# Two projections of a mixer on a seven-product scheme, woven between plain column groups, with four attention heads in one row

## The chip, the cores and the metric

The kernel runs on one core of one Trainium2 chip. The metric is device time in microseconds (us) of one execution, lower is better. The time of the kernel before is the median of three runs.

## The reference

One layer of an encoder with 256 tokens and a model width of 2048, all in float32:

```python
x = layer_norm(ALPHA * x + 0.5 * swiglu(x, ffn1_w1, ffn1_w3, ffn1_w2))
mix = hybrid_mixer(x, w_in, ...)
x = layer_norm(ALPHA * x + mix)
x = layer_norm(ALPHA * x + 0.5 * swiglu(x, ffn2_w1, ffn2_w3, ffn2_w2))
x = x + sigmoid(x @ w_ple_gate) * (p @ w_ple_proj)
```

The mixer multiplies x by one wide matrix `w_in` (2048 rows) and cuts the result into columns: q, k, v and the output gate of an mLSTM (1024 columns each, 4 heads of 256), 8 columns for the mLSTM's input and forget gates, q, k, v of a stick-breaking attention (1024 columns each, 8 heads of 128) and two merge gates (2048 columns each). The mLSTM's q and k go through a causal convolution over four tokens and a silu. Each mLSTM head forms decayed scores of 256 x 256 tokens, multiplies them by v, divides by a normaliser (the row sum of the scores, bounded below), normalises the head, and multiplies by the sigmoid of the output gate. Both branches are then projected up, gated, added and projected out.

## The kernel before

**Matmuls.** A float32 weight tile of 256 rows x 512 columns (512 KB, called raw) is loaded by SP's DMA queue, and split by ScalarE and VectorE into a high part (`nc.scalar.copy`, line 1024) and a low part (`nc.vector.tensor_tensor`, line 1028) of a reduced-precision type that TensorE multiplies fast. The activations, transposed, exist as high and low part too (`ActT`). A product of one weight tile with one half of the tokens is a `Unit`: for each of the tile's two blocks of 128 rows three matmuls of 128 x 512 (lines 1073 to 1075: high x high, high x low, low x high), so six matmuls for each unit.

**Plain groups.** `group` makes the units of one column group: 512 columns, 8 weight tiles over the 2048 rows, and each tile is used for both token halves, so 16 units, accumulated in two PSUM banks.

**Seven products.** `seven` (line 295) treats two column groups and two token halves and two row halves as a 2 x 2 block product and forms it by 7 products in place of 8, in Winograd's form. It needs sums of activation blocks (`act.forms`, made by `form_turn`, line 261), and sums of weight blocks. Some sums are made while loading, by a second DMA on POOL's queue that adds to the tile (line 1001), others by VectorE (`plus`, line 310). For 2048 rows it has 28 units, each with a weight tile of its own: products 1 and 2 first, with four units each, then four rounds of products 5, 7, 6, 4 and 3, whose five PSUM banks stay open over all four rounds. In the kernel before only the two feed-forward parts use it: 8 of their 11 chunks are made so (`up7`), and their units are woven (`weave`) between the plain units of the other work.

**The mixer.** Its projections are all plain groups, in this order: q group 0, the gates with the first two stick-breaking heads' q (264 columns), q group 1, k 0, k 1, v 0, v 1, output gate 0 and 1, then the stick-breaking columns in portions of 4, 4, 4, 4, 4 and 2 heads (`sb_columns`), the merge gates (`branch`), the two up-projections (`ups`), and the projection out. `conv` turns a finished q or k group: 4 transposes, then ScalarE's and VectorE's steps (line 690) that read PSUM. `sb_turn` (line 601) transposes a finished portion of stick-breaking q or k. `mlstm(h)` and `stick(h)` are the steps of one attention head. They are generators: each step is put into the engines' programs when its due time, counted in units already emitted, has come (`Sched`). The mLSTM's heads run as two sequences side by side, (0, 1) and (2, 3); a head waits for gates, q, k and v at its start, and for the output gate before its last steps (line 769). The row sum of the scores comes from a column of ones behind v: the matmul at line 754 has 257 columns.

**What sets the order.** Each engine runs its program in the order in which the Python code emitted it. The weights ahead of the matmuls are bounded by two numbers: raw tiles held (8 in the feed-forward parts, 5 in the mixer, 4 near a boundary) and split tiles held (6, near a boundary 11). Raw tiles, split halves, activations and the large intermediate values share one pool of 44 pages of 4 KB in each partition (`PAGES`); a raw tile takes one page, a split tile two. Short-lived values use 6 temporary buffers (`TEMP_BUFS`): if none is free, the code emits pending steps ahead of their due time. All matmul results use 8 PSUM banks (`PSUM_BUFS`).

Of the kernel before, what the change touches and what calls it, by code (L numbers as in the profile page):

```python
# [13 lines left out]
P = 128  # L14
S = 256
TT = S // P
D = 2048
# [120 lines left out]


class Boundary:  # L140


    def __init__(self, mixer):
        self.mixer = mixer


def weave(main, side):
# [22 lines left out]
def kernel(  # L170
# [121 lines left out]
                               i == 0, i == len(rows) - 1, done) for t in range(TT)])  # L292
        return pairs

    def seven(wa, wb, rows, col0, cols, act, done):

        n = rows // (4 * P)
        accs = {m: {} for m in range(1, 8)}

        def unit(m, i, tile, src, half, sub):
            return Unit(tile, half, accs[m], src, i, sub, i == 0, i == n - 1, lambda ps, t, m=m: done(m, ps))

        def plus(out, a, b):
            def make():
                nc.vector.tensor_tensor(out=out.tile[:, :, :cols], in0=a.tile[:, :, :cols], in1=b.tile[:, :, :cols],  # L310
                                        op=ALU.add)
            return make

        units = []
        for m, sub in ((1, 0), (2, 2)):
            for i in range(n):
                units.append(unit(m, i, plain(rows_of(wa, (4 * i + sub) * P, col0, cols)), act, 0, sub))
        for i in range(n):
            b11, b12, b22, b21 = (rows_of(w, (4 * i + sub) * P, col0, cols)
                                  for w, sub in ((wa, 0), (wb, 0), (wb, 2), (wa, 2)))  # L320
# [12 lines left out]
    program = []  # L333

    def boundary(mixer):
        program.append(Boundary(mixer))


    class Norm:
# [96 lines left out]
    def ffn(w1, w3, w2, act, norm, skew=True, ahead=()):  # L436
# [22 lines left out]
        def up7(c):  # L459
# [46 lines left out]
                return  # L506
                yield

            return seven(w1, w3, D, c * COL, COL, act, done)

        def down(*chunks):
            pairs = []
# [20 lines left out]
        boundary(True)  # L533


    xT = ActT(act_tile, ActT(act_tile))
# [13 lines left out]
    flags = set()  # L550

    def mixer_setup():
        st["sel"] = big()[0:HM, 0:HM * P].rearrange("q (h s) -> q h s", s=P)
        nc.vector.memset(st["sel"], 1.0)
        nc.gpsimd.affine_select(st["sel"], st["sel"], pattern=[[-1, HM], [0, P]], compare_op=ALU.is_equal,
                                fill=0.0, base=0, channel_multiplier=1)
        raw = temp()
        nc.sync.dma_start(out=raw[0:64, 0:P], in_=conv_m[0].rearrange("j (b q) -> (j b) q", q=P))
        st["cw"] = small.tile([P, 64], F32, name="cw", bufs=1)
        st["bi"] = small.tile([HM, 1], F32, name="bi", bufs=1)  # L560
        st["bf"] = small.tile([HM, 1], F32, name="bf", bufs=1)
        bg = b_gates_m[0].rearrange("(a h) -> a h", h=HM)
        nc.sync.dma_start(out=st["bi"][:], in_=bg[0].rearrange("(h o) -> h o", o=1))
        nc.sync.dma_start(out=st["bf"][:], in_=bg[1].rearrange("(h o) -> h o", o=1))

        def later():
            yield DELAY["gb"]
            ps = misc([P, 64])
            nc.tensor.transpose(ps[:], raw[0:64, 0:P], ident[0:64, 0:64])
            nc.vector.tensor_copy(out=st["cw"][:], in_=ps[:])  # L570
            drop()
            flags.add("cw")
        sched.spawn(later())
# [122 lines left out]
            yield DELAY["cv2"]  # L696
        drop(2)

    def v_done(g):
        def done(ps, t):  # L700
            st["v", t, g] = big()[:, 0:2 * (DM + 1)].rearrange("q (h d) -> q h d", d=DM + 1)
            nc.vector.memset(st["v", t, g][:, :, DM:], 1.0)
            nc.scalar.copy(st["v", t, g][:, :, 0:DM], ps.rearrange("q (h d) -> q h d", d=DM))
            flags.add(("v", t, g))
        return done
# [5 lines left out]
    def mo_done(g):  # L711
        def done(ps, t):
            if ("mo", t) not in st:
                st["mo", t] = big()
            cs = slice(g * COL, (g + 1) * COL)
            activate(st["mo", t][:, cs], ps, ACT.Sigmoid)
            nc.gpsimd.tensor_tensor(out=st["mo", t][:, cs], in0=st["mo", t][:, cs],
                                    in1=st["nm"][:, cs], op=ALU.mult)
            flags.add(("mo", t, g))
        return done  # L720

    ymT, ysbT = ActT(act_tile), ActT(act_tile)

# [1 line left out]
        return tl[:, 0:512].rearrange("q (a s) -> q a s", s=S)[:, :, 0:P]  # L725

    def mlstm(h):
        yield from wait("gates", ("qk", 0, h), ("qk", 1, h), ("v", 0, h // 2), ("v", 1, h // 2))
        d = temp()
        ps = misc([P, S])  # L730
        nc.tensor.matmul(ps[:], st["sel"][:, h], st["M"], start=True, stop=True)
# [18 lines left out]
        for t in range(TT):  # L750
            ps = misc([P, DM + 1])
            for s in range(t + 1):
                off = s * 256 + (t - s) * P
                nc.tensor.matmul(ps[:], d[:, off:off + P], st["v", s, h // 2][:, h % 2], start=(s == 0), stop=(s == t))  # L754
# [82 lines left out]
    first = 2  # L837
    for n in (4, 4, 4, 4, 4, 2):
        program.extend(flat(group(w_in, range(0, D, 2 * P), sq0 + first * DS, n * DS, x1T,
                                  lambda ps, t, f=first, n=n: sb_columns(ps, t, f, n))))  # L840
        first += n
        if first == 18:
            program.append(lambda: [sched.spawn(in_sequence([stick(a), stick(a + 2), stick(a + 4), stick(a + 6)]))
                                    for a in (0, 1)])


    mergedT = ActT(act_tile)
# [57 lines left out]
        if g == 1:  # L905
            program.append(norm2.load)

    boundary(False)


    x3T = ActT(act_tile)
# [55 lines left out]

    warm(WARM)

    weights, edges = [], []  # L970
    for u in program:
        if isinstance(u, Boundary):
            edges.append((len(weights), u.mixer))
# [6 lines left out]

    def limits(j):

        if any(-EDGE <= j - e < EDGE for e, _ in edges):
            return RAW_EDGE, SPLIT_EDGE
        mixer = [m for e, m in edges if e <= j][-1:] == [True]
        return (RAW_MIX, SPLIT_MIX) if mixer else (RAW_FFN, SPLIT_FFN)

    def pieces(j):
        return [slice(0, 1), slice(1, 2)] if j == 0 else [slice(0, 2)]
# [63 lines left out]
    splits_due()  # L1053
    warm(WARM2)
    for u in program:
        if isinstance(u, Boundary):
            continue
        if not isinstance(u, Unit):
            u()
# [51 lines left out]
```

## Time and profile before

| | |
|---|---|
| median of 3 runs | 2207.83 us (2206.65 to 2209.06) |
| the profiled execution | 2207.09 us, of which the span in the profile is 2205.4 us |
| TensorE's granted clock | 1.000 |
| TensorE matmul busy | 2196.6 us (100% of the span) |
| VectorE busy | 1747.1 us (79%) |
| ScalarE busy | 1244.5 us (56%) |
| GpSimd busy | 118.9 us (5%) |
| moved by DMA | 543.85 MB, mean 247 GB/s |

The profile lists engines as PE (matmul), PEld (TensorE's weight load), DVE (VectorE), ACT (ScalarE), POOL (GpSimd) and SP (the queue that issues most DMAs). Matmuls are pipelined: a row's duration is longer than the distance to the next one, and TensorE counts as busy when it only works below its peak. L1074 is line 1074 of the kernel.

### The profile page before, as it was taken

To read this page: it belongs to the slowest core of one execution; us is meant where nothing else is said; L and a number is where in the kernel's file an instruction comes from. 1 tells how busy PE (TensorE), PEld (TensorE's weight loads), DVE (VectorE), ACT (ScalarE), POOL (GpSimd) and SP (SyncE) were. 2 spreads that over 40 slices of the span, in tenths; PEclk is the share of its full clock that TensorE was granted. 3 is DMA by queue.
4 is the path that set the end of the run, shared out by engine and by line. 5 is a ranking of instruction groups with operands and counts; after the bars stand their busy time and mean duration, and the time that the engine had idled before them with its cause. 6 is when DMAs were issued, how large, how long until landed. Compare 5 with 4: busy or idle time off the path is not lost.

```text
span 2205.4 us, 27919 instructions
## 1 busy us (share of the span) xinstructions
PE 2196.6 (100%) x10062; PEld 1819.0 (82%) x10062; DVE 1747.1 (79%) x1923; ACT 1244.5 (56%) x1505; POOL 118.9 (5%) x111
## 2 busy tenths in 40 slices
PE   9999999999999999999999999999999999999999
PEld 7888888888888888888888888888888888887888
DVE  6999999999987874654445456699999999989774
ACT  7556656565655555545643344656565565656372
POOL 0100010000000000000100000000010001000000
PEclk9999999999999999999999999999999999999999
DMA  9899999999993765655566666579989999999553
GB/s 334 246 312 299 283 283 318 303 308 275 320 315 115 217 199 158 190 164 167 158 190 187 187 225 218 183 230 303 303 265 306 324 287 298 288 301 336 200 165 104
DMA packets 284811, 543.85 MB, mean 247 GB/s; under 512 B 17120, under 2 KB 26240, under 8 KB 284672
## 3 DMA queue, kind: packets, MB, share of 16 engines
q1 hardware_dynamic: 262912, 500.12, 68.3%
q0 software_dynamic: 21760, 41.95, 11.0%
q8 instruction: 79, 1.29, 0.2%
q14 instruction: 60, 0.49, 0.1%
HBM read 539.90 MB, written 2.10 MB: 246 GB/s over the span
## 4 chain that ended last, share of the span: by engine, by line
PE 94%; DVE 2%; DMA 2%; issue 1%; ACT 0%; SPq 0%; DVEq 0%; POOLq 0%; ACTq 0%
PE mm L1074 30%; PE mm L1073 30%; PE mm L1075 30%; DMA raw<-in_ffn_w_dram 2%; DVE split L1028 1%; PE ms L249 1%; PE ms L392 0%; DVE raw L310 0%; PE ms L791 0%; PE ms L814 0%; PE ms L742 0%; PE ms L754 0%; PE ms L804 0%; ACT split L1024 0%; DVE actT L256 0%
## 5 line engine op out<-in xcount | busy, mean ns | idle before, releaser
L1028 DVE TENSOR_TENSOR split<-raw,split 128x1024 fp32r<-128x1024 f32 (+1 forms) x1013 | 1177.6, 1201 | 237.8 <-ACT split L1024 225.3
L1024 ACT CAST split<-raw 128x1024 fp32r<-128x1024 f32 (+1 forms) x1013 | 1007.0, 1036 | 496.9 <-DVE raw L310 139.5
L1073 PE MATMUL mm<-split,actT 128*128 128x512 f32 (+2 forms) x3152 | 1226.9, 389 | 0.5 <-DVE xres L516 0.5
L1074 PE MATMUL mm<-split,actT 128*128 128x512 f32 (+2 forms) x3152 | 1215.1, 386 | 1.4 <-DVE split L1028 1.3
L1075 PE MATMUL mm<-split,actT 128*128 128x512 f32 (+2 forms) x3152 | 1215.1, 386 | 0.6 <-DVE actT L256 0.6
L1074 PEld LDWEIGHTS mm<-split,actT 128*128 128x128 f32 x3152 | 592.8, 188 | 120.3 <-DVE split L1028 6.1
L1075 PEld LDWEIGHTS mm<-split,actT 128*128 128x128 f32 x3152 | 592.2, 188 | 121.0 <-DVE actT L256 1.4
L1073 PEld LDWEIGHTS mm<-split,actT 128*128 128x128 f32 x3152 | 592.6, 188 | 117.0 <-issue 1.0
L310 DVE TENSOR_TENSOR raw<-raw 128x1024 f32<-128x1024 f32 x176 | 214.6, 1219 | 1.9
L1001 POOL DMA_DIRECT2D raw<-in_ffn_w_dram x80 | 95.9, 1198 | 1415.7 <-DMA raw<-in_ffn_w_dram 404.1
L251 ACT CAST actT<-ms 128x512 fp32r<-128x512 f32 x60 | 35.0, 585 | 89.4 <-PE ms L249 88.4
L463 DVE TENSOR_TENSOR temp<-mm,temp 128x512 f32<-128x512 f32 x112 | 76.7, 685 | 6.4 <-PE mm L1075 4.6
L516 DVE SCALAR_TENSOR_TENSOR xres<-mm,xres 128x512 f32<-128x512 f32 x96 | 65.3, 684 | 15.9 <-PE mm L1075 15.8
L256 DVE TENSOR_TENSOR actT<-ms,actT 128x512 fp32r<-128x512 f32 x60 | 40.9, 683 | 24.6 <-ACT actT L251 13.7
L221 ACT ACTIVATE big<-mm 128x512 f32<-128x512 f32 x20 | 12.0, 598 | 55.8 <-PE mm L1075 55.8
L221 ACT ACTIVATE temp<-temp 128x512 f32<-128x512 f32 (+1 forms) x48 | 28.5, 593 | 23.8 <-DVE temp L806 22.0
L221 ACT ACTIVATE temp<-mm 128x512 f32<-128x512 f32 (+1 forms) x22 | 12.3, 560 | 45.5 <-PE mm L1075 45.4
L217 ACT ACT_TABLE_LOAD x29 | 37.2, 1283 | 0.5
L244 DVE TENSOR_TENSOR actT<-temp,actT 128x512 fp32r<-128x512 f32 x32 | 21.4, 688 | 17.3 <-ACT actT L243 17.2
L861 DVE TENSOR_TENSOR big<-mm,big 128x512 f32<-128x512 f32 x16 | 11.1, 692 | 30.0 <-PE mm L1075 30.0
L690 DVE SCALAR_TENSOR_TENSOR temp<-ms,cw,temp 128x253 f32<-128x253 f32 (+2 forms) x48 | 23.1, 481 | 7.4 <-ACT temp L221 6.2
L221 ACT ACTIVATE rstd<-mv,eps 128x1 f32<-128x1 f32 x6 | 1.8, 295 | 46.4 <-DVE mv L375 46.4
(124 smaller groups left out, 542.1 us busy)
## 6 DMA issues: line engine op xcount, KB each, us to landing
raw<-in_ffn_w_dram SPq DMA_DIRECT2D x655, 512.0 KB, 6.5
raw<-in_w_in_dram SPq DMA_DIRECT2D x168, 512.0 KB, 3.8
raw<-in_ffn_w_dram POOLq DMA_DIRECT2D x80, 512.0 KB, 8.9
raw<-in_w_out_dram SPq DMA_DIRECT2D x32, 512.0 KB, 5.3
raw<-in_w_ple_gate_dram SPq DMA_DIRECT2D x24, 512.0 KB, 4.8
raw<-in_w_up_m_dram SPq DMA_DIRECT2D x16, 512.0 KB, 3.9
raw<-in_w_up_sb_dram SPq DMA_DIRECT2D x16, 512.0 KB, 4.4
raw<-in_w_ple_gate_dram SPq DMA_DIRECT2D x16, 256.0 KB, 4.4
```

The costliest lines, as they stand in the source:

```text
L217: nc.scalar.preload_act_table_set(table[0])
L221: nc.scalar.activation(out, in_, func, **kw)
L256: nc.vector.tensor_tensor(out=dst[:, 1], in0=ps[:], in1=dst[:, 0], op=ALU.subtract)
L310: nc.vector.tensor_tensor(out=out.tile[:, :, :cols], in0=a.tile[:, :, :cols], in1=b.tile[:, :, :cols], op=ALU.add)
L463: nc.vector.tensor_tensor(out=out, in0=a, in1=b, op=op)
L516: nc.vector.scalar_tensor_tensor(out=xs, in0=ps, scalar=0.5, in1=xs, op0=ALU.mult, op1=ALU.add)
L1001: nc.gpsimd.dma_start(out=r.tile[:, :, :r.cols], in_=r.plus, accum_op=ALU.add)
L1024: nc.scalar.copy(hi[:, ks], r[:, ks])
L1028: nc.vector.tensor_tensor(out=lo[:, ks], in0=r[:, ks], in1=hi[:, ks], op=ALU.subtract)
L1073: nc.tensor.matmul(ps, hi, w[0][:, k, :u.cols], start=first, stop=False)
L1074: nc.tensor.matmul(ps, hi, w[1][:, k, :u.cols], start=False, stop=False)
L1075: nc.tensor.matmul(ps, lo, w[0][:, k, :u.cols], start=False, stop=last)
```

## The change

The mLSTM's v and output gate are made by `seven`, each as one call for both of its column groups, in place of four plain groups. The 56 units are woven between the plain units of q 1, k 0, k 1 and the first three stick-breaking portions, in that ratio (96 to 56). For this the normalised activations `x1T` get the sums of blocks (`forms`), so the norm keeps whole copies of them. In this stretch 7 raw tiles are held in place of 5. `both7` combines the seven products into the result's four blocks, in pages of their own.

The mLSTM's four heads become one sequence, and each waits for its output gate at its start. Since v now lies in a page without room for the column of ones, the row sum comes from matmuls of their own with one column of `ones`, on the same scores. The selection matrix `sel` is replaced by a broadcast column of the identity.

```diff
-RAW_FFN, RAW_MIX, RAW_EDGE = 8, 5, 4
-SPLIT_FFN, SPLIT_MIX, SPLIT_EDGE = 6, 6, 11
+HELD = {"ffn": (8, 6), "mix": (5, 6), "wide": (7, 6)}
+RAW_EDGE, SPLIT_EDGE = 4, 11
...
-    def seven(wa, wb, rows, col0, cols, act, done):
+    def seven(wa, ca, wb, cb, rows, cols, act, done):
...
+    def both7(w, ca, cb, act, dest, ready):
+
+        r, held = {}, {}
+
+        def put(k, t, a, b, op):
+            nc.vector.tensor_tensor(out=r[k, t], in0=a, in1=b, op=op)
+
+        def rest():
+            u = r[0, 1]
+            put(0, 1, held[7], u, ALU.add)
+            z = r[1, 1] = dest(1, 1)
+            nc.vector.scalar_tensor_tensor(out=z, in0=u, scalar=-1.0, in1=held[5],
+                                           op0=ALU.mult, op1=ALU.subtract)
+            ready(1, 1)
...
+        def done(m, ps):
+            held[m] = ps
+            if m == 1:
+                r[0, 1] = dest(0, 1)
+                nc.scalar.copy(r[0, 1], ps)
+            elif m == 2:
+                r[0, 0] = dest(0, 0)
+                put(0, 0, ps, r[0, 1], ALU.add)
+                ready(0, 0)
+            elif m == 6:
+                r[1, 0] = dest(1, 0)
+                put(0, 1, ps, r[0, 1], ALU.add)
+                put(1, 0, held[5], r[0, 1], ALU.add)
+                sched.spawn(rest(), DELAY["rest"])
+            elif m == 4:
+                sched.until(lambda: (1, 1) in r)
+                put(0, 1, ps, r[0, 1], ALU.add)
+                ready(0, 1)
+            elif m == 3:
+                put(1, 0, ps, r[1, 0], ALU.subtract)
+                ready(1, 0)
+
+        return seven(w, ca, w, cb, D, COL, act, done)
...
-    x1T = ActT(act_tile)
+    x1T = ActT(act_tile, ActT(act_tile))
...
-        st["sel"] = big()[0:HM, 0:HM * P].rearrange("q (h s) -> q h s", s=P)
-        nc.vector.memset(st["sel"], 1.0)
-        nc.gpsimd.affine_select(st["sel"], st["sel"], pattern=[[-1, HM], [0, P]], compare_op=ALU.is_equal,
-                                fill=0.0, base=0, channel_multiplier=1)
...
+    def v_dest(g, t):
+        if ("v", t) not in st:
+            st["v", t] = big()
+        return st["v", t][:, g * COL:(g + 1) * COL]
...
+    def mo_ready(g, t):
+        a = mo_dest(g, t)
+        activate(a, a, ACT.Sigmoid)
+        nc.gpsimd.tensor_tensor(out=a, in0=a, in1=st["nm"][:, g * COL:(g + 1) * COL], op=ALU.mult)
+        flags.add(("mo", t, g))
...
     def mlstm(h):
-        yield from wait("gates", ("qk", 0, h), ("qk", 1, h), ("v", 0, h // 2), ("v", 1, h // 2))
+        yield from wait("gates", ("qk", 0, h), ("qk", 1, h), ("v", 0, h // 2), ("v", 1, h // 2),
+                        ("mo", 0, h // 2), ("mo", 1, h // 2))
...
-        nc.tensor.matmul(ps[:], st["sel"][:, h], st["M"], start=True, stop=True)
+        nc.tensor.matmul(ps[:], ident[0:HM, h:h + 1].broadcast_to([HM, P]), st["M"], start=True, stop=True)
...
-                nc.tensor.matmul(ps[:], d[:, off:off + P], st["v", s, h // 2][:, h % 2], start=(s == 0), stop=(s == t))
+                nc.tensor.matmul(ps[:, 0:DM], d[:, off:off + P], st["v", s][:, h * DM:(h + 1) * DM],
+                                 start=(s == 0), stop=(s == t))
+            for s in range(t + 1):
+                off = s * 256 + (t - s) * P
+                nc.tensor.matmul(ps[:, DM:], d[:, off:off + P], ones[:, 0:1], start=(s == 0), stop=(s == t))
...
-        yield from wait(("mo", 0, h // 2), ("mo", 1, h // 2))
...
+    program.append(load_norm_m)
+    program.append(lambda: sched.spawn(in_sequence([mlstm(a) for a in range(HM)])))
+    main = []
     for which, g in ((0, 1), (1, 0), (1, 1)):
-        program.extend(flat(group(w_in, range(0, D, 2 * P), which * 1024 + g * COL, COL, x1T, qk_done(which, g))))
-    program.append(load_norm_m)
-    program.append(lambda: [sched.spawn(in_sequence([mlstm(a), mlstm(a + 1)])) for a in (0, 2)])
-    for g in range(2):
-        program.extend(flat(group(w_in, range(0, D, 2 * P), 2048 + g * COL, COL, x1T, v_done(g))))
-    for g in range(2):
-        program.extend(flat(group(w_in, range(0, D, 2 * P), 3072 + g * COL, COL, x1T, mo_done(g))))
...
+        main += flat(group(w_in, range(0, D, 2 * P), which * 1024 + g * COL, COL, x1T, qk_done(which, g)))
...
+    for first in (2, 6, 10):
+        main += sb(first, 4)
+    side = (both7(w_in, 2048, 2048 + COL, x1T, v_dest, v_ready)
+            + both7(w_in, 3072, 3072 + COL, x1T, mo_dest, mo_ready))
+    mode("wide")
+    program.extend(weave(main, side))
+    mode("mix")
+    program.extend(sb(14, 4))
+    program.append(lambda: [sched.spawn(in_sequence([stick(a), stick(a + 2), stick(a + 4), stick(a + 6)]))
+                            for a in (0, 1)])
+    program.extend(sb(18, 4) + sb(22, 2))
```

More of the change, by code (lines that the diff above doesn't have):

```diff
@@ L140, with __init__ @@
 class Boundary:
-    def __init__(self, mixer):
-        self.mixer = mixer
+    pass
+class Mode:
+    def __init__(self, name):
+        self.name = name
 def weave(main, side):
@@ L316, in seven @@
             for i in range(n):
[L317 removed]
+                units.append(unit(m, i, plain(rows_of(wa, (4 * i + sub) * P, ca, cols)), act, 0, sub))
         for i in range(n):
[L319 to L320 removed]
+            b11, b12, b22, b21 = (rows_of(w, (4 * i + sub) * P, c, cols)
+                                  for w, c, sub in ((wa, ca, 0), (wb, cb, 0), (wb, cb, 2), (wa, ca, 2)))
             t1 = Raw(b12.src, cols, b11.src)
@@ L331, in seven, with mode, boundary @@
         return units
-    program = []
-    def boundary(mixer):
-        program.append(Boundary(mixer))
+    def both7(w, ca, cb, act, dest, ready):
[9 more added lines that the diff above has]
+            ready(1, 1)
+            return
+            yield
+        def done(m, ps):
[20 more added lines that the diff above has]
+        return seven(w, ca, w, cb, D, COL, act, done)
+    program = []
+    def mode(name):
+        program.append(Mode(name))
+    def boundary(name):
+        program.append(Boundary())
+        mode(name)
     class Norm:
@@ L507, in late @@
                 yield
-            return seven(w1, w3, D, c * COL, COL, act, done)
+            return seven(w1, c * COL, w3, c * COL, D, COL, act, done)
         def down(*chunks):
@@ L697, in conv, with v_ready @@
         drop(2)
[L699 to L705, printed above, removed]
+    def v_dest(g, t):
+        if ("v", t) not in st:
+            st["v", t] = big()
+        return st["v", t][:, g * COL:(g + 1) * COL]
+    def v_ready(g, t):
+        flags.add(("v", t, g))
     def load_norm_m():
@@ L709, in load_norm_m, with mo_dest @@
         nc.sync.dma_start(out=st["nm"][:], in_=norm_m[0].partition_broadcast(P))
[L711 to L720, printed above, removed]
+    def mo_dest(g, t):
+        if ("mo", t) not in st:
+            st["mo", t] = big()
+        return st["mo", t][:, g * COL:(g + 1) * COL]
+    def mo_ready(g, t):
[3 more added lines that the diff above has]
+        flags.add(("mo", t, g))
     ymT, ysbT = ActT(act_tile), ActT(act_tile)
@@ L906 @@
             program.append(norm2.load)
-    boundary(False)
+    boundary("ffn")
     x3T = ActT(act_tile)
@@ L968 @@
     warm(WARM)
-    weights, edges = [], []
+    weights, edges, modes = [], [], [(0, "ffn")]
     for u in program:
         if isinstance(u, Boundary):
-            edges.append((len(weights), u.mixer))
+            edges.append(len(weights))
+        elif isinstance(u, Mode):
+            modes.append((len(weights), u.name))
         elif isinstance(u, Unit) and u.tile.index is None:
@@ L981, in limits @@
     def limits(j):
-        if any(-EDGE <= j - e < EDGE for e, _ in edges):
+        if any(-EDGE <= j - e < EDGE for e in edges):
             return RAW_EDGE, SPLIT_EDGE
-        mixer = [m for e, m in edges if e <= j][-1:] == [True]
-        return (RAW_MIX, SPLIT_MIX) if mixer else (RAW_FFN, SPLIT_FFN)
+        return HELD[[m for e, m in modes if e <= j][-1]]
     def pieces(j):
```

15 lines of the change are left out of this document (5 added, 10 removed).

## The prediction

> **What bounds the kernel now.** I read the page first (span, engine totals, chain), then TensorE's timeline inside the mixer, then busy time by stage.
>
> ```profile
> span 2205.4 us, 27919 instructions
> PE 2196.6 (100%) x10062; PEld 1819.0 (82%) x10062; DVE 1747.1 (79%) x1923; ACT 1244.5 (56%) x1505; POOL 118.9 (5%) x111
> PE 94%; DVE 2%; DMA 2%; issue 1%; ACT 0%; SPq 0%; DVEq 0%; POOLq 0%; ACTq 0%
> ```
>
> The chain that ended last is TensorE's for 94%. TensorE's idle time is 2205.4 - 2196.6 = 8.8 us in all, so what removes work from it shortens the span, unless a wait takes its place. "Busy" is a weak measure, though, since durations overlap; the pace is the distance between starts:
>
> ```profile
> 754.63 0.39 PE L1075 MATMUL mm<-split,actT 128*128 128x512 f32 x1
> ...
> 756.89 0.39 PE L1073 MATMUL mm<-split,actT 128*128 128x512 f32 x1
> ```
>
> These are the first and the last of eleven rows of plain matmuls in the mixer: ten distances in 2.26 us, 0.226 us for a matmul of 512 columns. The second question is whether the other engines could feed a stretch of seven-product units in the mixer as they do in the feed-forward parts. Columns: window, its length, then busy time and count for PE, PEld, DVE, ACT and POOL, clock, DMA share, GB/s.
>
> ```profile
> 265.00:315.00 50.00, 49.65 (x224) 40.79 (x223) 45.57 (x47) 28.43 (x31) 3.58 (x3) 1.00 0.95 295
> 400.00:500.00 100.00, 100.00 (x449) 82.32 (x448) 94.64 (x96) 59.86 (x65) 7.15 (x6) 1.00 0.99 309
> 730.00:823.00 93.00, 93.00 (x459) 78.06 (x458) 75.76 (x108) 55.78 (x78) 0.00 (x0) 1.00 0.68 201
> 823.00:880.00 57.00, 57.00 (x254) 46.50 (x253) 26.79 (x46) 29.07 (x38) 1.84 (x3) 1.00 0.57 166
> 940.00:1000.00 60.00, 60.00 (x274) 49.71 (x273) 27.27 (x30) 20.27 (x26) 0.00 (x0) 1.00 0.55 160
> 1420.00:1450.00 30.00, 30.00 (x134) 24.82 (x133) 29.72 (x40) 21.35 (x28) 0.00 (x0) 1.00 0.71 228
> 1960.00:2060.00 100.00, 99.07 (x441) 80.66 (x441) 90.80 (x93) 59.53 (x64) 6.01 (x5) 1.00 0.95 312
> PE mm L1074 <- DVE split L1028: 0.9, 2, 0.6
> PEld mm L1074 <- DVE split L1028: 4.4, 9, 1.0
> ```
>
> In woven feed-forward work (400 to 500) VectorE is busy 0.946 and DMA moves 309 GB/s, and TensorE never idles. At the start of the second feed-forward part (1420 to 1450), where the sums of activations are made, VectorE is at 0.99 and TensorE still has no gap. The worst 100 us (1960 to 2060) cost TensorE 0.93 us, and another bad place (265 to 315) 0.35 us. The two wait rows, after 1420, name VectorE's splits: 0.9 us on matmuls, 4.4 us on weight loads, most of it under a running matmul. The mixer's windows have slack: VectorE 0.81, then 0.47 and 0.45.
>
> **What is removed.** v and the output gate take four plain groups of 16 units now, 64 units, and 56 after. Eight units of six matmuls: 48 x 0.226 = **-10.8 us** on TensorE. Nothing hides TensorE's work, so all of it is off the path. The selection matrix's memset and select, and the memsets of v's ones column, lie on VectorE and POOL in stretches with slack: nothing.
>
> **What is added on TensorE.** Each head has three score blocks that now also meet a single column of ones: 12 matmuls. A float32 matmul appears as two passes, each with its own weight load.
>
> ```profile
> 741.84 0.44 PE ms L632 x4
> 761.82 0.34 PE ms L654 x4
> 836.71 0.43 PE ms L754 x2
> 838.52 0.87 PE ms L754 x4
> ```
>
> The head's matmuls at line 754 have 257 columns: 0.87 / 4 = 0.218 us a pass, so a column is under 1 ns, and going from 257 to 256 gives back nothing. A one-column pass is bound by something else. The nearest row is line 654 with 4 columns and a load 128 wide: 0.34 / 4 = 0.085 us. Above it stands line 632 with 128 columns, 0.11 us. 24 passes x 0.085 = **+2.0 us**; ends 1.0 (half the nearest row, if a repeated load of the same scores overlaps better) and 2.6 us. [...] The broadcast identity column in place of `sel` keeps the matmul's shape: 0.
>
> **What is added on VectorE, and its cover.** The woven stretch has 96 + 56 units, 152 x 6 x 0.226 = 206 us, and some 5 us of transposes, so TensorE gives the others 211 us.
>
> ```profile
> L1028 DVE TENSOR_TENSOR split<-raw,split 128x1024 fp32r<-128x1024 f32 (+1 forms) x1013 | 1177.6, 1201 | 237.8 <-ACT split L1024 225.3
> L310 DVE TENSOR_TENSOR raw<-raw 128x1024 f32<-128x1024 f32 x176 | 214.6, 1219 | 1.9
> 303.79 2.27 DVE split L1028 x2
> L463 DVE TENSOR_TENSOR temp<-mm,temp 128x512 f32<-128x512 f32 x112 | 76.7, 685 | 6.4 <-PE mm L1075 4.6
> L690 DVE SCALAR_TENSOR_TENSOR temp<-ms,cw,temp 128x253 f32<-128x253 f32 (+2 forms) x48 | 23.1, 481 | 7.4 <-ACT temp L221 6.2
> L610 DVE COPY big<-ms 128x256 f32<-128x256 f32 x14 | 5.3, 416 | 3.4 <-PE ms L604 3.4
> L244 DVE TENSOR_TENSOR actT<-temp,actT 128x512 fp32r<-128x512 f32 x32 | 21.4, 688 | 17.3 <-ACT actT L243 17.2
> ```
>
> A split alone takes 1.20 us and a sum of weights 1.22, but back to back two take 2.27 (row 303.79): 1.135 each. Splits: 48 for the plain units, 56 for the others; sums of weights: 11 for each of the two calls, 22. 126 x 1.135 = 143 us. Three convolutions, 36 x 0.481 = 17. Combining products, 14 x 0.685 = 10. Turned stick-breaking columns, 12 x 0.416 = 5. The activations' sums: four chunks with four half-width operations and two splits each, at most 24 x 0.69 = 17, and half of them before the stretch begins. The norm's remaining scale and shift and the gates, some 10. Together 200 at most, 0.95 of 211: the load that the feed-forward rows carry at a cost of 0 to 0.9 us in 100 us. The cover is the six split tiles held ahead, about 8 us of TensorE's work; when it is used up, each further us of VectorE is a us of the span. I take **+0.8 us**, from the two bad windows, ends 0 and 2. ScalarE gets 24 casts more, about 25 us in 211, at half load: nothing.
>
> **Banks.** From the first round to the last, a call keeps five of the eight PSUM banks, the plain group two, so one is left for transposes. In the feed-forward parts these are spaced apart; in the mixer they are not.
>
> ```profile
> 785.04 0.44 PE ms L679 x4
> 792.30 0.44 PE ms L679 x4
> 958.75 0.44 PE ms L604 x4
> 960.59 0.44 PE ms L604 x4
> ```
>
> By the ratio of the weave, two events fall into rounds: k 0's convolution (the first two rows, heads 7.3 us apart) and the stick-breaking portion that has q and k columns (the last two rows: two transposed pieces each, now without a gap). The convolution holds its bank for six VectorE steps of 0.48 and two ScalarE steps, some 5 us, less than 7.3: nothing. In the other, the second piece must wait until VectorE has copied the first (0.42, behind a split of up to 1.2): about 0.8 us, twice or three times, and behind it on TensorE stand all later matmuls. **+1.5 us**, ends 0 and 5.
>
> **DMA, pages.** The stretch loads 48 + 58 tiles of 0.524 MB in 211 us, 263 GB/s, below the 309 of the feed-forward window. Ten of the loads are POOL's added ones.
>
> ```profile
> raw<-in_w_in_dram SPq DMA_DIRECT2D x168, 512.0 KB, 3.8
> raw<-in_ffn_w_dram POOLq DMA_DIRECT2D x80, 512.0 KB, 8.9
> 273.09 8.64 DMA raw<-in_ffn_w_dram
> 282.38 9.21 DMA raw<-in_ffn_w_dram
> ```
>
> A summed tile needs 3.8 us and then 8.9 (last column). Seven raw tiles ahead are 7 x 211 / 106 = 14 us, so the chain of 12.7 fits. Counting pages at the start of the second call's rounds gives 8 + 8 for activations, 19 for weights ahead, 4 q and k, 3 or 4 stick-breaking, 4 v and output gate, 2 others: up to 48 of 44, so for some 40 us loads wait for pages and 3 or 4 tiles are ahead. Two DMA waits of 8.6 and 9.2 us in a row in the chain (273 to 292) cost TensorE only the 0.35 us of the window 265 to 315; cost here 0, upper end 2 us.
>
> **The heads in one row.**
>
> ```profile
> 740.52 0.16 ACT L623 COPY gst<-mm 128x8 f32<-128x8 f32 x1
> 885.49 0.62 PE ms L731 x2
> 908.04 0.44 PE ms L779 x4
> 1001.43 1.31 PE ms L791 x8
> 1104.69 1.31 PE ms L814 x8
> L861 DVE TENSOR_TENSOR big<-mm,big x16: 691/692/692, 1148.2 to 1315.6; 128x512 f32<-128x512 f32 x16
> ```
>
> The stretch begins where the gates' group is done, at 740.5 (its first copy, line 623), and ends 211 us later, about 952. A head takes 885.5 to 908.5, 23 us; four of them from 952 end near 1044. The sticks start where the stretch's next group ends, 22 us on (96 matmuls), at 974, earlier than now, and take 104 us (1001.4 to 1106.0): to about 1078. Their first use is the up-projection before line 861's first row, now at 1148: over 40 us to spare. Heads and sticks now share the 6 temporary buffers (2 + 4 at most, and two staged portions at the start), which may bring one step forward, 0 to 1 us; I add 0.1 us. The wait for the output gate moves from a head's end to its start; it holds up emission only, no queue.
>
> **Sum.** -10.8 + 2.0 + 0.8 + 1.5 + 0.1 = -6.4 us. Against the profiled execution (2207.09 = span 2205.4 + 1.7 around it) that is 2200.7; the median of the runs lies 0.74 higher, so **2201.4 us**. By the ends: -10.8 + 1.0 = -9.8 with no stall, 2198.0; -10.8 + 2.6 + 2 + 3 = -3.2 at the pessimistic end, where not every bound is reached at once, 2204.6. About 0.2%, 4.4 us, is what a measurement of this kernel can tell from no change.
>
> **Rivals.**
>
> *One bank and a saturated VectorE give the gain back.* For: 0.95 load without the slack of a mean; the stretch's first half holds three convolutions and the activations' sums, so its load is above the mean, and TensorE waits in order. Against: 1420 to 1450 at 0.99 with no gap. The bank waits at their end of 5 us and 2 to 4 us of late splits: -10.8 + 2.0 + 5 + 3 = about -1 us, 2207.
>
> *Late sums make it slower.* Mechanism: pages run out, raw tiles ahead fall, and each tile that POOL's DMA completes comes late; ScalarE and VectorE wait in order behind it. It decides from the point where raw tiles ahead (2.0 us each) and split tiles (about 8 us) cover less than 12.7 + 2.3 us of load and split: under 3.5 raw tiles. Then the second call's five summed tiles, and the splits behind them, would each expose about 3 us, 15 us: -6.4 + 15 = +9, 2217. For: the page count above. Against: the feed-forward chain at 273 to 292, and its DMA share of 0.99. [...]
>
> *The removed matmuls were not the limit,* so that the woven stretch runs at a slower pace per matmul and part of the saving isn't there; at half of it -5.4 + 4.4 = -1, 2207. Against: the same pace, 0.22 to 0.23 us counting transposes, in 400 to 500 (449 instructions in 100 us).
>
> **How the numbers follow.** Forecast 0.76, of which 0.02 lie above 2203.4; gain given back 0.10, not the limit 0.04, late sums 0.10. Faster by over 0.2%: 0.76 - 0.02 = 0.74. Within: 0.02 + 0.10 + 0.04 = 0.16. Slower: 0.10. The range runs from 2197.5 (no stall, and the runs' scatter) to 2206.5, which takes in the first rival's milder half.
>
> **What would show it.** Right: 48 fewer matmuls on lines 1073 to 1075, line 754's successor with 24 one-column passes, VectorE near 0.9 in the woven stretch with TensorE idle under 3 us there, heads over before 1060, first up-projection 5 to 8 us earlier. Wrong: TensorE waiting for VectorE's split or copy by more than 5 us between 740 and 952, POOL's DMA in the chain there, or a transpose at line 604 or 679 waiting for its bank.

## The result, and the profile after

The changed kernel takes 2233.0 us (median of 4 runs, 2231.0 to 2233.7), beside 2208.4 us for the kernel before: ratio 1.011, 95% interval 1.0093 to 1.0128. It is 24.6 us slower, where 6.4 us faster was forecast, and lies above the range of 2197.5 to 2206.5 us.

The page of the changed kernel: span, engine totals, and the chain that ended last by engine.

```profile
span 2230.0 us, 28110 instructions
PE 2202.2 (99%) x10038; PEld 1818.8 (82%) x10038; DVE 1818.6 (82%) x2002; ACT 1273.2 (57%) x1535; POOL 126.5 (6%) x120
PE 90%; DVE 4%; DMA 3%; issue 2%; ACT 1%; SPq 0%; DVEq 0%; POOLq 0%; ACTq 0%
```

TensorE's share of the chain fell from 94% to 90%, and its idle time grew from 8.8 to 2230.0 - 2202.2 = 27.8 us. The removed work is gone (3136 matmuls on each of the three lines, before 3152: 48 fewer), yet TensorE is busy 5.6 us longer. The loss is all in the mixer. From the norm's first transposes (697.9, before 695.2) to the last row of the projection out (1433.0, before 1406.3) the mixer takes 735.1 us, before 711.1.

The view of waits, for TensorE in the mixer of the changed kernel: the waiting instruction, what it waited for, us in total, times, longest.

```profile
PE ms L800 <- DVE temp L790: 5.0, 2, 3.1
PE ms L724 <- ACT temp L712: 4.0, 1, 4.0
PE mm L1129 <- DVE split L1083: 3.5, 3, 2.7
PE mm L1128 <- ACT split L1079: 2.8, 1, 2.8
PE mm L1128 <- DVE big L655: 1.8, 1, 1.8
PE ms L649 <- DVE big L655: 1.2, 1, 1.2
```

Line 724 is a convolution's transposes, 800 a head's value matmul, 649 the transposes of stick-breaking columns. None of the rows names a DMA. The same view of the kernel before shows no wait of TensorE in the mixer (695 to 1406) at all. Next the view of windows for the first 60 us of the woven stretch. Columns as in the prediction: window, length, PE, PEld, DVE, ACT, POOL where there is any, clock, DMA share, GB/s. The changed kernel, all its work:

```profile
740.00:800.00 60.00, 49.15 (x188) 37.39 (x187) 54.33 (x80) 31.79 (x45) 2.38 (x2) 0.86 0.65 190
```

The same window of the changed kernel, instructions that touch split tiles alone:

```profile
740.00:800.00 60.00, 47.15 (x172) 35.68 (x171) 25.24 (x22) 22.03 (x23) 0.86 0.65 190
```

The kernel before, all its work:

```profile
740.00:800.00 60.00, 60.00 (x280) 49.40 (x279) 52.30 (x74) 36.08 (x52) 0.00 (x0) 1.00 0.66 191
```

And its split tiles alone:

```profile
740.00:800.00 60.00, 58.36 (x252) 46.49 (x251) 28.61 (x25) 23.97 (x25) 1.00 0.66 191
```

The woven stretch needs 104 split tiles for its 152 units, where plain units would need 76. But VectorE made 22 in 60 us, before 25; 54.3 - 25.2 = 29.1 us of its time went to other things, before 23.7. New among these other things are the sums of activations with their splits (9.1 us by the view of lines, lines 248 and 270 to 274) and sums of weights (3.7 us, line 314); scale and shift take 9.6 us in both kernels. And TensorE's clock in this window is 0.86. Six rows of the changed kernel's timeline, merged by time from its three engines, show how a wait comes about. Columns: start, length, engine, line, operation; in brackets the idle time ahead of it and what ended it.

```profile
755.01 0.46 DVE L682 TENSOR_SCALAR big<-ms,bf 4x256 f32<-4x256 f32 x1
755.56 0.42 ACT L225 ACTIVATE big<-big 4x256 f32<-4x256 f32 x1 [6.25 <-DVE big L682]
756.00 1.28 ACT L221 ACT_TABLE_LOAD   x1
758.15 3.87 ACT L1079 CAST split<-raw 128x1024 fp32r<-128x1024 f32 x4
759.21 1.23 DVE L1083 TENSOR_TENSOR split<-raw,split 128x1024 fp32r<-128x1024 f32 x1 [3.74 <-ACT split L1079]
759.23 0.80 PE L1128 MATMUL mm<-split,actT 128*128 128x512 f32 x1 [2.82 <-ACT split L1079]
```

VectorE reaches the gates' step at line 682 late, since splits, scale and shift and the sums of activations stand before it. ScalarE, next in its own order at a gate step, stands still for 6.25 us with casts of weights queued behind. VectorE then has no cast to subtract from and waits 3.74 us, and TensorE, out of split weights, 2.82 us. Such a chain alone doesn't stop TensorE, though. In the kernel before ScalarE stands at the same step too, in the view of waits from 740 to 800, and TensorE doesn't wait:

```profile
ACT big L221 <- DVE big L637: 4.9, 1, 4.9
```

The view of windows again, in steps of 5 us of the changed kernel, for the clock (the third column from the end):

```profile
755.00:760.00 5.00, 2.18 (x8) 1.12 (x6) 1.26 (x3) 4.38 (x6) 1.19 (x1) 0.88 0.84 193
760.00:765.00 5.00, 4.54 (x12) 3.54 (x12) 4.93 (x11) 3.85 (x6) 0.00 (x0) 0.50 0.33 58
790.00:795.00 5.00, 1.00 (x4) 0.53 (x4) 5.00 (x6) 2.42 (x4) 0.00 (x0) 0.80 1.02 287
795.00:800.00 5.00, 5.00 (x15) 4.00 (x14) 4.35 (x7) 2.52 (x5) 0.00 (x0) 0.52 1.00 326
```

After these two waits, of 2.82 and 3.98 us, TensorE runs at about half clock for some 5 us (0.50 and 0.52). Over the execution the granted clock is 0.995 (before 1.000): 0.005 x 2230 = 11 us of clock, part of it during idle time. The length of the wait alone does not tell whether this happens: it followed one of 2.82 us here, and the last section shows one of 3.08 us after which the clock stayed at 1.00.

### The profile page after: what moved, and what is told of

Same layout as the page of the kernel before. It is cut to its first block, busy times and chain, and to the rows that moved or that the text cites. A ratio compares the mean times of both kernels' runs of the same rounds, so it can differ in the third digit from the quotient of the medians.

```text
span 2230.0 us, 28110 instructions
## 1 busy us (share of the span) xinstructions
PE 2202.2 (99%) x10038; PEld 1818.8 (82%) x10038; DVE 1818.6 (82%) x2002; ACT 1273.2 (57%) x1535; POOL 126.5 (6%) x120
## 4 chain that ended last, share of the span: by engine, by line
PE 90%; DVE 4%; DMA 3%; issue 2%; ACT 1%; SPq 0%; DVEq 0%; POOLq 0%; ACTq 0%
PE mm L1128 29%; PE mm L1129 29%; PE mm L1130 29%; DVE split L1083 2%; DMA raw<-in_ffn_w_dram 1%; PE ms L253 1%; DMA raw<-in_w_in_dram 1%; ACT split L1079 1%; PE ms L441 0%; DVE raw L314 0%; PE ms L800 0%; DVE actT L248 0%; PE ms L840 0%; PE ms L863 0%; PE ms L853 0%
## 5 line engine op out<-in xcount | busy, mean ns | idle before, releaser
L1083 DVE TENSOR_TENSOR split<-raw,split 128x1024 fp32r<-128x1024 f32 (+2 forms) x1037 | 1211.4, 1205 | 201.6 <-ACT split L1079 192.4
L1079 ACT CAST split<-raw 128x1024 fp32r<-128x1024 f32 (+2 forms) x1037 | 1034.0, 1036 | 553.6 <-DVE raw L314 144.5
L314 DVE TENSOR_TENSOR raw<-raw 128x1024 f32<-128x1024 f32 x198 | 241.7, 1221 | 3.4 <-DMA raw<-in_ffn_w_dram 1.0
L915 DVE TENSOR_TENSOR big<-mm,big 128x512 f32<-128x512 f32 x16 | 11.1, 692 | 30.0 <-PE mm L1130 30.0
L1056 POOL DMA_DIRECT2D raw<-in_w_in_dram x10 | 11.9, 1192 | 320.9 <-DVE big L682 145.6
L247 ACT CAST actT<-temp 128x512 fp32r<-128x512 f32 x32 | 19.4, 622 | 15.9 <-DVE temp L271 15.1
```

Of the source, the lines that this page charges most:

```text
L1056: nc.gpsimd.dma_start(out=r.tile[:, :, :r.cols], in_=r.plus, accum_op=ALU.add)
L1079: nc.scalar.copy(hi[:, ks], r[:, ks])
L1083: nc.vector.tensor_tensor(out=lo[:, ks], in0=r[:, ks], in1=hi[:, ks], op=ALU.subtract)
```

## The experiments

A row's line number is that of the run's own kernel: edits that add lines ahead of the mixer shift them by 11 (649, 724 and 800 here are then 660, 735 and 811). The ratios are to the kernel before, run again beside each set of runs (medians 2208.9 to 2209.4 us); gains in us are differences of the medians.

Theory A: VectorE's queue. Around the start of the woven stretch its work exceeds the time, and since ScalarE and VectorE work in order and wait for each other (6.25 and 3.74 us in the rows above), TensorE waits for both. Theory B: raw tiles come late, through page shortage or POOL's adding loads.

**Scale and shift later.** The norm's `affine` steps and their vectors' pages go behind the stretch:

```diff
-            sched.spawn(self.affine(t, c), self.wait[0] + self.wait[1] * (2 * c + t))
+            if not self.apart:
+                sched.spawn(self.affine(t, c), self.wait[0] + self.wait[1] * (2 * c + t))
...
-    program.extend(branch(0, 0) + branch(0, 1) + branch(1, 0) + branch(1, 1))
-    program.extend(ups(0) + ups(1))
+    program.extend(branch(0, 0) + branch(0, 1) + branch(1, 0))
+    program.append(lambda: norm1.scale_half(0))
+    program.extend(branch(1, 1))
+    program.extend(ups(0))
+    program.append(lambda: norm1.scale_half(1))
+    program.extend(ups(1))
```

> The changed kernel, with the first norm's scale and shift (16 VectorE operations of 0.69 us, now between 744 and 790) moved behind the woven stretch, where VectorE is half idle; the pages of its two vectors are loaded there too, so that four pages fewer are held at the stretch's start. Theory A (VectorE's backlog at the start of the woven stretch makes TensorE wait, and the low clock after each wait adds to it): 16 x 0.65 = 10 us of VectorE's work leave the place where each us counts, so 2233 - 10 = 2223, and with less time at the low clock down to 2218; TensorE's idle time between 740 and 800 falls from about 11 us to under 5. Theory B (raw tiles come late, by page shortage or by POOL's adding loads): under 3 us gained, 2230 or more, unless the four pages are what was missing, in which case the waits of ScalarE's casts for loads fall and not those for VectorE.

2221.9 us, ratio to before 1.0058 (1.0043 to 1.0073): 11.1 us gained for some 10 us of VectorE's work, as theory A has it. The view of windows of this run: VectorE's share hardly moves, but TensorE's does (55.4 us busy, 49.2 in the changed kernel).

```profile
740.00:800.00 60.00, 55.40 (x235) 43.21 (x234) 53.91 (x78) 38.22 (x53) 2.38 (x2) 0.94 0.66 199
```

**The same, with the pages held.** At the old places two copies of one column each read the vectors, which are loaded at the old place and again later.

> As the kernel with scale and shift moved later (2222), but the four pages of the norm's vectors are loaded and held as in the changed kernel: at each old place of a scale and shift stand two copies of one column (about 0.1 us each) that read them; the vectors are loaded again behind the stretch. Tells VectorE's work from the pages, which both left the stretch's start in that run. Theory A (VectorE's work): 16 x 0.1 = 2 us come back at most, 2221 to 2226. Pages: the gain of 11 us is gone, 2230 to 2234.

2223.9 us, 1.0063 (1.005 to 1.0077). Most of the gain stays (9.2 of 11.1 us), so it came from VectorE's work and not from four free pages. The same window of this run:

```profile
740.00:800.00 60.00, 54.54 (x233) 42.65 (x233) 53.92 (x89) 36.57 (x51) 2.38 (x2) 0.94 0.71 211
```

**Without the added loads.**

```diff
-        return seven(w, ca, w, cb, D, COL, act, done)
+        units = seven(w, ca, w, cb, D, COL, act, done)
+        for u in units:
+            for raw in u.tile.loads:
+                raw.plus = None
+        return units
```

> The changed kernel without the ten loads that POOL's queue adds to the raw tiles of v and the output gate: those weight sums are left out, everything else is done. Theory A: only the late place at 917 to 940 (waits of 4.4 and 10.0 us for loads in the chain) changes, 1 to 4 us, 2229 to 2232. Theory B: the waits in the whole stretch go with them, 2205 to 2218.

The kernel leaves ten weight sums out, so its v and output gate hold other values. 2231.7 us, 1.01 (1.0085 to 1.0116): 1.4 us, which is not clear of the scatter. Late loads are in the chain of the changed kernel in the second call's rounds (two of its rows: start, us, load):

```profile
916.83 4.44 DMA raw<-in_w_in_dram
921.83 9.98 DMA raw<-in_w_in_dram
```

Behind them in that chain stand VectorE's splits and its copy of a finished bank (line 655), for which TensorE waited 1.8 us at 943.7. Without the added loads no load is in the chain from 895 to 950, and TensorE's wait there is:

```profile
PE mm L1132 <- DVE big L659: 0.3, 1, 0.3
```

So the added loads cost 1.5 us at this place. They have no part in the loss from 740 to 800: TensorE is busy 48.3 us there without them, 49.2 with them.

**Five raw tiles.** `"wide": (5, 6)` in place of `(7, 6)`.

> The changed kernel with 5 raw tiles held in the woven stretch in place of 7. If the shortage of pages costs time (up to 48 wanted of 44), two pages fewer help: 2222 to 2228. If the lookahead of the loads is what binds (12.7 us for a summed tile), it gets worse: 2237 to 2245. Theory A: neither binds, 2230 to 2236.

2243.8 us, 1.0159 (1.0145 to 1.0173): 10.8 us worse. ScalarE's casts now wait for loads (36.1 us, 4.5 in the changed kernel), as the waits of all engines from 740 to 980 show for this run:

```profile
ACT split L1079 <- DMA raw<-in_w_in_dram: 36.1, 7, 9.6
```

And TensorE, in its waits through the mixer, for the splits:

```profile
PE mm L1129 <- DVE split L1083: 7.5, 8, 2.7
PE mm L1128 <- ACT split L1079: 5.3, 4, 2.8
```

So theory B's mechanism is real at five tiles and is held off at seven. I had expected theory A to exclude it; it doesn't. More than seven was not tried.

**Gates later.** `"g0": 110.0` in place of `3.0`, so that the gate steps fall into the middle of the stretch.

> The changed kernel, with the mLSTM's gate steps (now at 745 to 786) started 110 us of emitted matmuls after their columns are ready in place of 3; nothing needs them before the heads, at about 970. Theory A in its narrow form (ScalarE stands 6.25 us behind a gate step that waits for VectorE, and VectorE then 3.7 us behind ScalarE): 2233 - 6 = 2227, down to 2222 with the clock, and ScalarE's idle time at 749 to 755 is gone. Theory A in its wide form (only VectorE's amount of work counts): the gates' 4 us leave the place, 2229. Theory B: no change, 2231 to 2234.

2230.1 us, 1.0089 (1.0071 to 1.0108): 2.9 us, near the wide form's number, but its interval overlaps that of the changed kernel (1.0093 to 1.0128), so alone the move is not clear of no gain. The profiled execution is the fastest of the four (2224.6 us, the others 2229.7 to 2231.4). In it the wait moved with the gates: a new one of 2.9 us stands before the transposes at line 649.

**Both moves.**

> Both moves at once. Theory A: 2213 to 2219, TensorE idle under 3 us between 740 and 860, and what is left over the 2201 of my forecast lies behind 900 (a late added load, a bank, the heads). Theory B: 2228 or more.

2217.3 us, 1.0045 (1.0026 to 1.0065), in the range of theory A: 4.6 us less than with scale and shift alone, though these two intervals overlap. What is left of TensorE's waits in the mixer of this run:

```profile
PE ms L811 <- DVE temp L801: 5.0, 2, 3.1
PE ms L660 <- ACT temp L654: 2.7, 1, 2.7
PE ms L660 <- DVE big L666: 1.1, 1, 1.1
```

The convolution's 4.0 us are down to 0.8, but the gates' wait at 890 is there (line 660, 2.7 us), and the heads' (line 811, 5.0 us).

**Gates behind the stretch.** The same with `"g0": 200.0`.

> As the kernel with both moves (2217), but the gate steps begin 200 us of emitted matmuls after their columns, that is behind the woven stretch; the heads follow them. Theory A, wide form (VectorE's amount of work): 4 us of VectorE's work at 0.85 load leave the stretch, up to 1 us gained, 2216. Theory A, narrow form (ScalarE and VectorE stand behind each other wherever the gate chain falls into a stretch with a full VectorE): the wait of 2.7 us before the transposes at 890 and the low clock behind it go, 2211 to 2214.

2211.8 us, 1.0012 (1.0003 to 1.0021). 5.5 us for about 4 us of VectorE's steps, and the 2.7 us wait is gone, as the narrow form had it; the wide form gave 1 us at most. But the heads moved along, and their wait fell too, from 5.0 to 2.8 us, while 1.8 us at line 839 are new. So from scale and shift alone to here the gates' move gained 10.1 us, clear of the scatter. That this chain costs more than its own 4 us because it passes between ScalarE and VectorE fits, but was not separated from the heads.

**Heads and turns.** Two more edits:

```diff
-    "m1": 0.6
+    "m1": 3.0
...
-                sched.spawn(sb_turn(name, t, stage, lo - 8 * which, hi - lo), DELAY["sbt"])
+                sched.spaced(sb_turn(name, t, stage, lo - 8 * which, hi - lo), DELAY["sbt"], TURN_GAP)
```

> As the one with the gates behind the stretch, and two more edits: a head leaves 3.0 us in place of 0.6 between its scores' scaling and the matmul that reads them, and the transposes of stick-breaking columns keep 3.4 us apart. If the late waits are what is left (5.0 us of TensorE before the heads' value matmuls, 1.8 us for a PSUM bank at 928 to 932), both rows vanish and the time falls by 5 to 8 us, to 2204 to 2209. If these waits only stand in front of others (VectorE full in any case), under 3 us.

2202.2 us (median of 10, 2200.8 to 2206.9), 0.9969 (0.996 to 0.9978): faster than the kernel before by 0.31%, and faster than the 2204 to 2209 expected. The profiled execution is the slowest of the ten (2206.9 us): it reaches the mixer at 700.4 us, the profiled one of the kernel before at 695.2, so the two are compared by the mixer alone. TensorE's waits in the mixer that are left:

```profile
PE ms L735 <- ACT temp L723: 0.8, 2, 0.6
PE ms L660 <- DVE big L666: 0.2, 1, 0.2
```

The waits of 5.0 us are gone. The view of windows, with the clock at 1.00:

```profile
740.00:800.00 60.00, 59.22 (x276) 48.66 (x276) 57.84 (x77) 38.65 (x52) 3.57 (x3) 1.00 0.80 238
910.00:970.00 60.00, 59.80 (x274) 49.01 (x273) 42.68 (x46) 31.72 (x39) 6.25 (x5) 1.00 0.83 263
```

VectorE is busier in the first 60 us than in the changed kernel (57.8 against 54.3) while TensorE runs: the rows of its split tiles have 30 instructions there, 33.5 us, where the changed kernel had 22. The gain of 9.7 us is more than the waits that the run before still had for heads, sticks and bank, 2.8 + 1.8 + 0.9 us; how much of the rest is the low clock, and how the gain divides between the two edits, was not separated. The four moves were not tried on the kernel before; TensorE has no wait in its mixer that they could remove.

**The weave later, alone.** `main[:32] + weave(main[32:], side)` in the changed kernel.

> The changed kernel with no other move, but the first 32 plain units (q 1 and k 0) go ahead unwoven, and the 56 units are woven into the 64 that are left. The work is the same on each engine. Theory A (a burst at the start: norm, gates, sums of activations and convolutions come on top of the doubled splits): the burst meets the lower load of plain units as in the kernel before, so the waits between 740 and 800 go, 14 us, and come back in part because the weave is denser: 2216 to 2223. If VectorE's total over the stretch is what binds, the place makes no difference: 2230 to 2236.

2235.5 us, 1.0124 (1.0105 to 1.0144): no gain. My expectation was wrong about what fills VectorE. Here the stretch begins with plain units only. The view of windows of this run, all work:

```profile
742.00:780.00 38.00, 29.30 (x125) 22.87 (x124) 34.21 (x55) 19.26 (x31) 0.00 (x0) 0.87 0.44 142
```

And split tiles alone:

```profile
742.00:780.00 38.00, 27.02 (x109) 21.09 (x108) 14.47 (x12) 11.02 (x12) 0.87 0.44 142
```

VectorE is busy 34.2 of 38 us, with 14.5 us on splits. The other 20 us are the sums of activations, scale and shift, the gates and a convolution. So the burst is there without the additional splits. Two rows of the timeline show one way in which it reaches TensorE: ScalarE stands 7.05 us for the sums of activations (line 271), and the copy for a convolution (line 712), queued behind, comes so late that TensorE waits 6.99 us for it.

```profile
770.66 1.29 ACT L247 CAST actT<-temp 128x512 fp32r<-128x512 f32 x2 [7.05 <-DVE temp L271]
773.43 1.39 PE L724 MATMUL ms<-ident,temp 128*128 128x128 f32 x4 [6.99 <-ACT temp L712]
```

In the kernel before this place was already nearly full (52.3 of 60 us) and had no such sums; that they tip it over is the reading which agrees with all runs here, but no run took those sums away alone.

**All moves, with the later weave.**

> All moves: scale and shift later, gates behind the stretch, heads' delay, spaced turns, and the weave begun after 32 plain units. If place is all that counts, nothing is left of the waits, and the forecast's arithmetic holds: 2200 to 2204. If the denser weave saturates VectorE, 2206 to 2212, with waits for splits between 840 and 950.

2208.0 us, 0.9993 (0.9984 to 1.0003), the second case: the denser weave gives 6 us back. The waits lie elsewhere than I had written, though: a PSUM bank (3.2 us at line 660) behind loads of 6.6 and 9.1 us in the chain, and half clock after it (for some 5 us the chain's matmuls stand 0.43 us apart, 0.23 before and later).

**Sums spread.** The four chunks' sums start 12 in place of 5 us apart.

> The changed kernel, with the sums of the norm's activations (four chunks, 3 us of VectorE each, due 18, 23, 28 and 33 us after their chunk) spread to 18, 30, 42 and 54. No work is taken away. Theory A: VectorE's work between 740 and 780 falls by some 6 us and comes after it, where the load is 0.9: 2224 to 2230. If what is left behind 780 is as full, nothing is gained: 2231 to 2235.

2230.1 us, 1.0093 (1.0078 to 1.0109): 2.9 us, at the upper edge of what A gave, and not clear of the scatter. VectorE's busy time did not fall by 6 us: it is 25.3 of 30 us from 740 to 770 and 29.1 of 30 behind, where the changed kernel has 25.2 and 29.1. What was moved met a stretch as full.

**Spread on top of the moves.**

> As the kernel with scale and shift later, gates behind the stretch, heads' delay and spaced turns (2202.2), and the activations' sums spread too. Its trace still has 0.8 us of waiting for a copy at 776 and some tenths for splits: theory A gives 2200 to 2202; if those tenths come from elsewhere, 2202 to 2203.

2202.7 us, 0.9971 (0.9962 to 0.9981): the same as without. The best version is the one with the four moves, and this one is no better.

## Why the prediction was wrong, point by point

- **What is removed** (-10.8): the 48 matmuls are gone, and the time can be seen once the waits are: with the moves the mixer takes 704.9 us, 6.2 less than before. By the terms, -10.8 + 2.0 and the 1.0 us of waits that are left, it would be 7.8 less; the other 1.6 us were not followed up.
- **The column of ones** (+2.0): right. Four passes take 0.34 us, 0.085 each, as in the row that I took:

```profile
1011.93 0.34 PE ms L804 x4
```

- **VectorE and its cover** (+0.8): this step failed. The total was about right: with the four moves VectorE is busy 187.2 us from 740 to 952, and scale and shift and the gates, some 15 us, would come on top; 200 was forecast. But I divided it by the whole stretch. From 740 to 800, scale and shift, gates, a convolution and the activations' sums come at once, and TensorE ran out of split weights (waits of 2.82 and 2.69 us): in place of 0.8 us it lost 60 - 49.15 = 10.9 us in this window, and ran at a clock of 0.86. "ScalarE: nothing" failed with it: at half load it still stood 6.25 us behind one late VectorE step, with all casts behind it, and the convolution's transposes waited 3.98 us for its copy. The window 1420 to 1450, which I took for proof that 0.99 does no harm, was no match. It lies in the 36 plain units ahead of the weave: VectorE sums no weights there (the next row of line 310 is at 1470.2), and 14 splits were enough for its 22 units. It isn't the lack of a chain that saved it, for ScalarE stood 7.0 us for the activations' sums there too:

```profile
L243 ACT CAST actT<-temp 128x512 fp32r<-128x512 f32 x4 | 2.5, 622 | 7.1 <-DVE temp L267 7.0
```

  The runs put the price at 11.1 us for scale and shift and 10.1 us for the gates (with what the heads gained by following them), low clock included.
- **The low clock** is in no term of my sum. Each wait was priced at its length; by the granted clock (0.995, before 1.000) it cost up to 11 us.
- **Banks** (+1.5): right in kind and place. The two rows add up to 1.8 + 1.2 = 3.0 us, but 1.5 us of it go with the added loads: without these the rows are 0.3 and 1.2 us.
- **Pages, late sums** (0, upper end 2): within its ends, 1.4 us without the added loads. A shortage of pages in the second call's rounds was not tested by itself.
- **Heads in one row** (+0.1, "holds up emission only, no queue"): this step failed too. I looked at when the row ends and not at the steps inside a head, which come 0.6 us apart: VectorE's scaling of the scores stood behind splits in its queue, and the value matmuls waited for it in two heads, 3.08 us at 982.4 and 1.88 us at 1066.3, 5.0 us in place of 0.1.
- **The rivals:** "one bank and a saturated VectorE" named the cause and gave it 8 us; the moves won back 30.8 us, heads and low clock included. The slower rival, late sums, was another mechanism, and at seven raw tiles not the one. POOL's only work in the window 740 to 800 is 2.4 us for two issues of added loads, without which the loss there was no smaller (TensorE 48.3 us busy, 49.2 with them); the output gate's multiplications stand between 903.1 and 982.7 us.
- **What would show it wrong** came as written: TensorE waits of more than 5 us for VectorE and ScalarE in the woven stretch, and the columns' transposes wait for their bank.

The steps add up: from 2233.0, -11.1 (scale and shift), -4.6 and -5.5 (gates), -9.7 (heads and turns) lead to 2202.2. These are differences of consecutive runs, so they add up by construction, and each holds for this order only: alone the gates' move gained 2.9 us. That the end lies 0.8 us from the forecast of 2201.4 is in part luck, since the moves are no part of the forecast's sum.

## What to carry to other kernels

An engine's load has to be summed in the windows in which its work falls due, some 30 to 60 us here, and not over a stretch; its mean of 0.95 hid a place where 10 us of movable work cost 11 us. Look for chains that pass between two in-order engines: moving one of about 4 us out of a stretch that was still full after the first move, with the heads behind it, gained 10.1 us; moved alone, and within the stretch, it gained 2.9 us, which the scatter does not let tell from nothing. Before a change that saves work on the critical engine is given up, its late helpers are worth moving: the same change lost 24.6 us and, with four moves, won 0.31%.

## What the runs showed of the hardware that was not expected

A wait of some 3 us can cost TensorE more than its length, but its length alone did not tell whether it does. In the changed kernel 2.82 us of waiting were followed by 5 us at a clock of 0.50, 3.98 us by 5 us at 0.52. The heads' wait of 3.08 us was followed by 0.75 there, in the window 985 to 990. In the kernel with both moves the same wait, just as long, cost nothing more (the wait's row, and the view of windows around it):

```profile
982.43 0.70 PE L800 MATMUL ms<-big,temp 128*128 128x256 f32 x2 [3.08 <-DVE temp L790]
985.00:990.00 5.00, 5.00 (x22) 4.25 (x21) 3.20 (x13) 2.46 (x4) 0.00 (x0) 0.75 0.47 120
966.53 0.70 PE L811 MATMUL ms<-big,temp 128*128 128x256 f32 x2 [3.08 <-DVE temp L801]
965.00:970.00 5.00, 3.47 (x19) 3.05 (x20) 3.41 (x7) 3.06 (x5) 1.29 (x1) 1.00 0.33 105
970.00:975.00 5.00, 5.00 (x28) 4.15 (x28) 3.43 (x10) 3.10 (x5) 0.00 (x0) 1.00 0.62 191
```

And with scale and shift moved later, TensorE's longest wait from 740 to 800 was 1.5 us, and its clock in that window was 0.94. In the five executions of the kernel with both moves the time goes with the clock, from 2215.2 us at 1.000 to 2224.8 us at 0.997.

And an engine with 0.91 of its time busy (VectorE, 54.3 of 60 us) made fewer splits than one at 0.87 in the kernel before, with 29.1 us of its time on other work (before 23.7) and a wait of 3.74 us for ScalarE between them. A busy share alone did not tell how much of the needed work got done.
